# Hybrid layer on one core: state space outputs made transposed, with z as columns and one norm a group

## The chip, the core and the metric

The kernel runs on one core of a Trainium2 chip. Time is device time in microseconds (us), the median of several runs. The engines are TensorE (PE; PEld is its weight load), VectorE (DVE), ScalarE (ACT), GpSimd (POOL) and SyncE (SP), which issues most of the transfers (DMA). Each engine works through its own queue in the order of the program.

## What is computed

One layer over 512 latent tokens and 256 context tokens with 1024 channels: a combined projection, a branch of gated linear attention (GLA, 4 heads), a branch of state space (SSD, 32 heads of 64 channels in 4 groups, chunks of 128 tokens), a merge with gates, and an FFN. The change is in the SSD branch. Cut to that branch, the reference is:

```python
# _ssd_scan, per chunk; a second scan runs backward, and the two outputs are added
cum = jnp.cumsum(ai, axis=1)
seg = cum[:, :, None] - cum[:, None, :]
Lm  = jnp.exp(jnp.where(mask, seg, -jnp.inf))
cb  = jnp.einsum('btgn,bsgn->btsg', ci, bi)
y   = jnp.einsum('btsg,btsge,bsgep->btgep', cb, Lm, xi)
y   = y + jnp.einsum('btgn,bgenp->btgep', ci, S) * jnp.exp(cum)[..., None]
S_new = jnp.exp(cum[:, -1])[..., None, None] * S + ...
# _mixer
o_b = o_b + d_skip * xh
o_b = o_b * silu(z)
o_b = rms_norm(o_b in 4 groups of 512, ssm_norm_w)
y_b = o_b @ w_pb
```

## The kernel before

Weights come by SP's DMA as fp32 and are split into a high part (whi, by ACT, L188) and the rest (wlo, by POOL or DVE, L189). A projection is three matmuls for each block of 128 inputs: whi with the activations' high part, wlo with the high part, whi with the low part. `proj_cols` gives channels on partitions (512 tokens in a row, banks l_ for latents and c_ for context), `proj_rows` gives tokens on partitions (256 channels in a row, banks r_). These banks have the tag mm, four in all; the chains use four others (tag sm).

The SSD branch is done in four groups g. `ssd_proj(g)` projects bm, cm and four blocks of xs with `proj_cols`, puts each through a convolution (cv_ on ACT and DVE, ct_ for its silu) and transposes it to rows (tr_b, tr_x on PE). Then z: in two column halves c, `proj_rows` makes four tiles of 128 tokens, 192 matmuls of 256 columns a group; ACT and DVE write silu(z) into the four tiles z[0] to z[3].

`ssd_chain(g)` makes the states and then, for each chunk n of 128 tokens, the outputs of the group's 8 heads:
- E: the transposed decay matrix of a head, four heads to a tile. SP broadcasts the cumulated decays from DRAM (cdr), DVE adds a bias for each direction (L830), a masked copy joins the two directions (L832), ACT takes the exp (L833), DVE multiplies by cb = B C (L840).
- y: 8 matmuls, E as the weights and 64 columns of x, into one bank (tokens on partitions). yi: two matmuls of 512 columns for what comes from the states ahead and behind.
- DVE scales each yi by exp(cum) and adds it to a tile that POOL made of x and gam (own term and skip, L851), adds the bank and multiplies by z.
- The norm of the chunk: square with its sum on ACT, power on POOL, product with the norm's weights snw on DVE (L866), four transposes on PE (yT), and out of their bank the high part yH by ACT (L871) and the low part yL by DVE (L872).

Order: the matmuls of the chains go through `Early`, which gives them high priority; the scheduler puts them between the matmuls of the projections. Chain g runs beside `ssd_proj(g+1)`, chain 3 beside the gate projections ga and gb. `proj_back` (pb) of a group follows its chain.

## Time and profile before

| | |
|---|---|
| median of three runs | 1442.92 us (1441.3 to 1446.59) |
| the profiled execution | 1443.79 us |
| its span | 1442.0 us |
| mean granted PE clock | 0.981 |
| PE, DVE, ACT, POOL busy | 94%, 61%, 34%, 33% |

The SSD branch lies between about 440 and 990 us. In a timeline a row has the start, the duration, the engine and the line, what is written from what, and in square brackets the idle time ahead of it with what ended it. A matmul's record is longer than the distance to the next one's start, since matmuls are pipelined; where a projection runs without holes, the distance between starts is what one costs. A line that ends in x6 is six instructions in a row.

### The profile page before, as it was taken

Reading aid. Unit: us, or ns where it says so; the run is one execution under the profiler, and the core shown is the slowest. Engines: PE = TensorE matmul, PEld = TensorE weight load, DVE = VectorE, ACT = ScalarE, POOL = GpSimd, SP = SyncE. Lnnn points to the kernel's source line nnn. Section 1 sums busy time; section 2 is a strip of 40 time slices with the busy share of each in tenths; the row PEclk is TensorE's granted clock in tenths of the full one; section 3 lists DMA queues with packets and bytes.
Section 4 is the critical chain, followed back from the end, with each engine's and each line's share of the span. In section 5 each row is a group of like instructions: output and inputs, shape, how many; then the busy total and the mean of one; then the engine's idle time right before and its main releaser. Section 6 shows DMA issues by size and latency. Waiting matters only on the chain.

```text
span 1442.0 us, 19130 instructions
## 1 busy us (share of the span) xinstructions
PE 1357.0 (94%) x7461; PEld 1149.3 (80%) x7461; DVE 882.6 (61%) x1316; ACT 497.1 (34%) x825; POOL 475.3 (33%) x340
## 2 busy tenths in 40 slices
...
GB/s 370 118 264 148 134 88 128 106 103 111 124 78 66 142 103 89 96 88 88 110 74 88 88 110 102 179 179 283 171 88 97 94 102 91 100 102 88 103 103 72
DMA packets 71354, 175.48 MB, mean 122 GB/s; under 512 B 6368, under 2 KB 22880, under 8 KB 71136
## 3 DMA queue, kind: packets, MB, share of 16 engines
...
## 4 chain that ended last, share of the span: by engine, by line
PE 62%; DVE 16%; DMA 11%; issue 5%; POOL 3%; ACT 2%; SPq 0%; POOLq 0%; DVEq 0%; ACTq 0%
DMA E<-cdr 7%; PE gate L1067 3%; PE gate L1068 3%; PE gate L1066 3%; PE up L1067 3%; PE up L1068 3%; PE up L1066 3%; PE db L206 3%; PE db L204 3%; PE db L205 3%; DVE E L830 2%; PE lv L577 2%; PE pb_pb L716 1%; PE pb_pb L715 1%; PE pb_pb L717 1%
## 5 line engine op out<-in xcount | busy, mean ns | idle before, releaser
L341 POOL TENSOR_TENSOR raw_ada<-raw_ada,cs 128x1024 f32<-128x1024 f32 x32 | 67.6, 2113 | 159.4 <-DMA raw_ada<-in_wts_dram 109.2
L170 POOL TENSOR_TENSOR rr_f<-rv_f,negh 128x1 f32<-128x1 f32 x4 | 2.6, 646 | 355.3 <-DVE rv_f L168 355.3
L830 DVE TENSOR_TENSOR E<-E,ebias 128x512 f32<-128x512 f32 x64 | 66.3, 1038 | 56.2 <-DMA E<-cdr 56.0
L386 PE MATMUL r_z<-whi_z,hH 128*128 128x256 f32 x256 | 74.5, 291 | 5.8 <-DVE cv_x L746 3.5
L343 POOL TENSOR_TENSOR raw_ada<-raw_ada 128x512 f32<-128x512 f32 x64 | 78.5, 1227 | 3.0
L388 PE MATMUL r_z<-whi_z,hL 128*128 128x256 f32 x256 | 73.2, 286 | 0.0
L387 PE MATMUL r_z<-wlo_z,hH 128*128 128x256 f32 x256 | 72.9, 285 | 0.0
L1067 PE MATMUL gate<-h2L,whi_gate 128*128 128x512 f32 (+1 forms) x192 | 72.0, 375 | 0.7 <-DVE h2L L1039 0.7
L1066 PE MATMUL gate<-h2H,whi_gate 128*128 128x512 f32 (+1 forms) x192 | 72.3, 377 | 0.0
L1068 PE MATMUL gate<-h2H,wlo_gate 128*128 128x512 f32 (+1 forms) x192 | 71.9, 374 | 0.0
L189 DVE TENSOR_TENSOR wlo_gate<-raw_gate,whi_gate 128x1024 fp32r<-128x1024 f32 x20 | 24.5, 1225 | 73.8 <-ACT whi_gate L188 73.8
L189 POOL TENSOR_TENSOR wlo_xs<-raw_xs,whi_xs 128x1024 fp32r<-128x1024 f32 x16 | 41.2, 2573 | 74.3 <-ACT whi_xs L188 74.3
L1066 PE MATMUL up<-h2H,whi_up 128*128 128x512 f32 x160 | 62.2, 389 | 0.0
L1067 PE MATMUL up<-h2L,whi_up 128*128 128x512 f32 x160 | 62.2, 389 | 0.0
L1068 PE MATMUL up<-h2H,wlo_up 128*128 128x512 f32 x160 | 62.2, 389 | 0.0
L189 DVE TENSOR_TENSOR wlo_down<-raw_down,whi_down 128x1024 fp32r<-128x1024 f32 x18 | 22.0, 1225 | 62.4 <-ACT whi_down L188 62.3
L833 ACT ACTIVATE E<-E 128x512 f32<-128x512 f32 x32 | 20.2, 632 | 112.0 <-DVE E L832 87.8
L1075 DVE TENSOR_TENSOR f<-f,up 128x512 f32<-128x512 f32 x22 | 15.1, 688 | 69.2 <-PE up L1068 68.5
L386 PE MATMUL r_v<-whi_v,hH 128*128 128x256 f32 x192 | 56.8, 296 | 0.0
L189 POOL TENSOR_TENSOR wlo_z<-raw_z,whi_z 128x1024 fp32r<-128x1024 f32 x16 | 39.7, 2484 | 49.1 <-ACT whi_z L188 39.4
L387 PE MATMUL r_v<-wlo_v,hH 128*128 128x256 f32 x192 | 55.8, 291 | 0.0
L388 PE MATMUL r_v<-whi_v,hL 128*128 128x256 f32 x192 | 55.8, 291 | 0.0
...
## 6 DMA issues: line engine op xcount, KB each, us to landing
...
E<-cdr SPq DMA_DIRECT2D x64, 256.0 KB, 3.6
...
```

The lines of the kernel that those rows point to most:

```text
L189: (nc.gpsimd if split_pool[0] else nc.vector).tensor_tensor(lo, raw, hi.bitcast(F32), ALU.subtract)
L204: nc.tensor.matmul(out_, aH, bH, start=start, stop=False)
L205: nc.tensor.matmul(out_, aH, bL, start=False, stop=False)
L341: nc.gpsimd.tensor_tensor(raw, raw, cs[:, :, 0:1].to_broadcast([P, KD, P]), ALU.mult)
L343: nc.gpsimd.tensor_tensor(raw[:, 0:n, :], raw[:, 0:n, :], raw[:, n:2 * n, :], ALU.add)
L386: nc.tensor.matmul(o, hH[:, kk, tk], hi[:, k, :], start=st, stop=False, skip_group_check=True)
L387: nc.tensor.matmul(o, hH[:, kk, tk], lo[:, k, :], start=False, stop=False, skip_group_check=True)
L388: nc.tensor.matmul(o, hL[:, kk, tk], hi[:, k, :], start=False, stop=sp, skip_group_check=True)
L830: nc.vector.tensor_tensor(ed, ed, ebias[:, d, n, hh].unsqueeze(2).to_broadcast([P, EH, P]), ALU.add)
L1066: nc.tensor.matmul(pts[kj][:, tk], hi[:, k, :], h2H[:, k, tk], start=(k == 0), stop=False)
L1067: nc.tensor.matmul(pts[kj][:, tk], hi[:, k, :], h2L[:, k, tk], start=False, stop=False)
L1068: nc.tensor.matmul(pts[kj][:, tk], lo[:, k, :], h2H[:, k, tk], start=False, stop=(k == KD - 1))
```

## The change

- z is projected with `proj_cols` in four blocks of 128 channels, 96 matmuls of 512 columns a group, into one tile of 128 x 4 x 512 with a single buffer (tag z). GLA and the last norm, which used the four buffers of that tag, use quarters of one such tile.
- The outputs are made transposed: channels on partitions. x (or a state) is the weight with 64 columns, E is what streams, 128 tokens wide. Even heads of a pair go to columns 0 to 63 of PE, odd heads to 64 to 127; two heads so fill a 128 x 128 block of the bank.
- What comes from the states is summed in the same bank: cd = exp(cum) C, made by ACT (exp of the broadcast decays) and POOL (product with C), streams against the states. Three buffers (tag cd).
- gam, now with both directions' dt, is put on E's diagonal by a second masked copy, with the mask id8.
- z is multiplied in place by the bank. The square sums over 512 channels are four matmuls with a column of ones (ss). The power, the diagonal matrix dg, the matmul that spreads the norms over the partitions (rrow), the product with the weights and the writing of yH and yL are done once a group, after its last chunk.

```diff
-        z = [ch.tile([P, 512], F32, tag="z", name=f"z_{g}_{i}", bufs=4) for i in range(4)]
-        for c in range(2):
-            banks = proj_rows(lambda kh: ("z", g, c, kh), 4)
-            for i in range(4):
-                pv = banks[i // 2][:, (i % 2) * 256:(i % 2) * 256 + 256]
-                zv = z[i][:, c * 256:(c + 1) * 256]
-                nc.scalar.activation(zv, pv, AF.Tanh, scale=0.5)
-                nc.vector.scalar_tensor_tensor(zv, zv, 1.0, pv, ALU.add, ALU.mult)
+        z = ch.tile([P, 4, SEQ], F32, tag="z", name=f"z_{g}")
+        for j in range(4):
+            lat, _ = proj_cols(("z", g, j), False)
+            nc.scalar.activation(z[:, j, :], lat, AF.Tanh, scale=0.5)
+            nc.vector.scalar_tensor_tensor(z[:, j, :], z[:, j, :], 1.0, lat, ALU.add, ALU.mult)
...
+        def square_sums(n):
+            sq = s2(f"sq{n}")
+            nc.scalar.activation(sq.rearrange("p (j t) -> p j t", t=P), z[:, :, n * P:(n + 1) * P], AF.Square)
+            pt = sm_bank(f"ss_{g}_{n}")
+            for j in range(4):
+                early.matmul(pt[:, 0:1], sq[:, j * P:(j + 1) * P], one, start=(j == 0), stop=(j == 3))
+
+            nc.vector.tensor_scalar(rv4[:, n:n + 1], pt[:, 0:1], 1.0 / (4 * 512), EPS, ALU.mult, ALU.add)
...
+                    cd = ch.tile([P, EH, P], F32, tag="cd", name=f"cd_{g}_{n}_{hf}_{d}", bufs=3)
+                    nc.scalar.activation(cd, ed, AF.Exp)
+                    nc.gpsimd.tensor_tensor(cd, cd, bc[:, 1, tk].unsqueeze(1).to_broadcast([P, EH, P]), ALU.mult)
                     nc.vector.tensor_tensor(ed, ed, ebias[:, d, n, hh].unsqueeze(2).to_broadcast([P, EH, P]), ALU.add)
...
+                nc.vector.copy_predicated(Eh[hf], id8.unsqueeze(1).to_broadcast([P, EH, P]),
+                                          gam[:, hf * EH:(hf + 1) * EH].unsqueeze(2).to_broadcast([P, EH, P]))
...
-            for e_ in range(HPG):
-                early.matmul(py[:, e_ * 64:(e_ + 1) * 64], Eh[e_ // EH][:, e_ % EH, :], xt[:, n, e_ * 64:(e_ + 1) * 64],
-                                 start=True, stop=True)
-            y = s2(f"y{n}")
-            nc.gpsimd.tensor_tensor(v8(y), v8(xt[:, n, :]), b8(gam), ALU.mult)
-            for d, S in ((0, Sf), (1, Sb[n])):
-                pi = sm_bank(f"yi_{g}_{n}_{d}")
-                early.matmul(pi, bc[:, 1, tk], S, start=True, stop=True)
-                yi = s2(f"yi{n}{d}")
-                nc.vector.tensor_tensor(v8(yi), v8(pi), b8(ecum[:, d, n, hs]), ALU.mult)
-                nc.vector.tensor_tensor(y, y, yi, ALU.add)
-            nc.vector.tensor_tensor(y, y, py, ALU.add)
-            nc.vector.tensor_tensor(y, y, z[n], ALU.mult)
+            for hf, term in ((0, 0), (0, 1), (1, 0), (1, 1), (0, 2), (1, 2)):
+                for eh in range(EH):
+                    e_ = hf * EH + eh
+                    es = slice(e_ * 64, (e_ + 1) * 64)
+                    w, m = ((xt[:, n, es], Eh[hf]), (Sb[n][:, es], Ch[hf][1]), (Sf[:, es], Ch[hf][0]))[term]
+                    early.matmul(py[64 * (e_ % 2):64 * (e_ % 2) + 64, (e_ // 2) * P:(e_ // 2 + 1) * P], w, m[:, eh, :],
+                                 start=(term == 0 and e_ < 2), stop=(term == 2 and e_ >= HPG - 2), skip_group_check=True)
...
-            ss = sml.tile([P, 1], F32, tag="ss", name=f"yss_{g}_{n}", bufs=4)
-            nc.scalar.activation(py, y, AF.Square, accum_out=ss)
-            r = rstd_of(ss, 4 * 512, f"y{g}{n}")
-            nc.vector.scalar_tensor_tensor(y, y, r, snw, ALU.mult, ALU.mult)
-            pt = sm_bank(f"yT_{g}_{n}")
-            for j in range(4):
-                early.transpose(pt[:, j * P:(j + 1) * P], y[:, j * P:(j + 1) * P], ident)
-            pv = pt.rearrange("p (j t) -> p j t", t=P)
-            nc.scalar.activation(yH[:, :, tk], pv, AF.Copy)
-            nc.vector.tensor_tensor(yL[:, :, tk], pv, yH[:, :, tk].bitcast(F32), ALU.subtract)
+            nc.vector.tensor_tensor(z[:, :, tk], py.rearrange("p (j t) -> p j t", t=P), z[:, :, tk], ALU.mult)
+            if n > 0:
+                square_sums(n - 1)
+        square_sums(NCH - 1)
+
+        r4 = sml.tile([P, NCH], F32, tag="rr4", name=f"rr_y{g}")
+        nc.gpsimd.tensor_tensor(r4, rv4, negh, ALU.pow)
+        dg = s2("dg")
+        nc.vector.tensor_tensor(dg.rearrange("p (n t) -> p n t", t=P), ident.unsqueeze(1).to_broadcast([P, NCH, P]),
+                                r4.unsqueeze(2).to_broadcast([P, NCH, P]), ALU.mult)
+        pr_ = sm_bank(f"rrow_{g}")
+        early.matmul(pr_, mkr[:, M_ONE - 1, :].bitcast(F32), dg, start=True, stop=True)
+        for j in range(4):
+            zj = z[:, j, :]
+            nc.vector.scalar_tensor_tensor(zj, zj, vecs[:, V_SN + 4 * g + j:V_SN + 4 * g + j + 1], pr_, ALU.mult, ALU.mult)
+            nc.scalar.activation(yH[:, j, :], zj, AF.Copy)
+            nc.vector.tensor_tensor(yL[:, j, :], zj, yH[:, j, :].bitcast(F32), ALU.subtract)
```

How the order moves, at three places. First PE at chunk 1 of group 1 (y_1_1), between the context matmuls of xs_2_0 (c_xs; st is a state's input, ss square sums of chunk 0, cb the next chunk's B C). Before:

```order
L368 MATMUL c_xs_2_0_6150<-hH_91,wlo_xs_2_0_6144 128x256
L364 MATMUL c_xs_2_0_6150<-hH_91,whi_xs_2_0_6143 128x256
L365 MATMUL c_xs_2_0_6150<-hL_92,whi_xs_2_0_6143 128x256
L577 MATMUL y_1_1_5845<-x_1_5017,E_1_1_0_1_5822 128x64 x2
L577 MATMUL yi_1_1_0_5856<-S_f1_1_5802,bc_1_4897 128x512
L577 MATMUL y_1_1_5845<-x_1_5017,E_1_1_0_1_5822 128x64
L577 MATMUL yi_1_1_1_5861<-S_b1_1_5730,bc_1_4897 128x512
L577 MATMUL y_1_1_5845<-x_1_5017,E_1_1_0_1_5822 128x64
L577 MATMUL y_1_1_5845<-x_1_5017,E_1_1_1_1_5830 128x64 x4
L368 MATMUL c_xs_2_0_6150<-hH_91,wlo_xs_2_0_6144 128x256
L364 MATMUL c_xs_2_0_6150<-hH_91,whi_xs_2_0_6143 128x256
```

and after the change:

```order
L578 MATMUL y_1_1_5683<-E_1_1_0_1_5643,x_1_4947 64x128 x2
L578 MATMUL st_1_f2_5708<-xc_f2_0_1_5709,bt_1_4897 128x512
L578 MATMUL y_1_1_5683<-E_1_1_0_1_5643,x_1_4947 64x128
L578 MATMUL ss_1_0_5718<-one_80,sq0_1_5716 128x1
L578 MATMUL y_1_1_5683<-E_1_1_0_1_5643,x_1_4947 64x128
L578 MATMUL cb_1_2_5738<-bc_1_4827 128x128
L578 MATMUL y_1_1_5683<-cd_1_1_0_1_5645,S_b1_1_5551 64x128
L578 MATMUL ss_1_0_5718<-one_80,sq0_1_5716 128x1
L578 MATMUL y_1_1_5683<-cd_1_1_0_1_5645,S_b1_1_5551 64x128
L578 MATMUL ss_1_0_5718<-one_80,sq0_1_5716 128x1
L578 MATMUL y_1_1_5683<-cd_1_1_0_1_5645,S_b1_1_5551 64x128
L578 MATMUL ss_1_0_5718<-one_80,sq0_1_5716 128x1
```

The block was one; now its first eight matmuls (half hf = 0, four heads, two terms; seven of them stand above) have six others between them, and the other sixteen come later.

Second, PE from chain 0's last chunk (y_0_3) to the transposes of group 1 (tr_b, tr_x). Before, from y_0_3 to the z matmuls (r_z) that follow:

```order
L577 MATMUL y_0_3_4859<-x_0_3890,E_0_3_0_1_4836 128x64 x2
L577 MATMUL yi_0_3_0_4870<-S_f3_0_4816,bc_0_3770 128x512
L577 MATMUL y_0_3_4859<-x_0_3890,E_0_3_0_1_4836 128x64
L577 MATMUL yi_0_3_1_4875<-S_b3_0_4591,bc_0_3770 128x512
L577 MATMUL y_0_3_4859<-x_0_3890,E_0_3_0_1_4836 128x64
L577 MATMUL y_0_3_4859<-x_0_3890,E_0_3_1_1_4844 128x64 x4
L386 MATMUL r_z_1_0_0_1_5335<-whi_z_1_0_0_5336,hH_91 128x256
L387 MATMUL r_z_1_0_0_1_5335<-wlo_z_1_0_0_5337,hH_91 128x256
```

and, 50 rows of r_z later:

```order
L387 MATMUL r_z_1_0_0_1_5335<-wlo_z_1_0_1_5391,hH_91 128x256
L388 MATMUL r_z_1_0_0_1_5335<-whi_z_1_0_1_5390,hL_92 128x256
L577 MATMUL yT_0_3_4889<-idt_77,y3_0_4868 128x128 x4
L757 MATMUL tr_b_1_0_4968<-idt_77,ct_b_1_4963 128x128 x4
L757 MATMUL tr_b_1_1_4974<-idt_77,ct_b_1_4963 128x128 x2
L757 MATMUL tr_x_1_0_0_5086<-idt_77,ct_x_1_0_5083 128x128 x4
L386 MATMUL r_z_1_1_0_0_5452<-whi_z_1_1_0_5454,hH_91 128x256
```

After the change, from the end of y_0_3:

```order
L578 MATMUL y_0_3_4766<-cd_0_3_1_0_4758,S_f3_0_4714 64x128 x4
L578 MATMUL ss_0_3_4802<-one_80,sq3_0_4800 128x1 x4
L578 MATMUL rrow_0_4812<-dg_0_4810,mkr_76 128x512
L759 MATMUL tr_b_1_0_4898<-idt_77,ct_b_1_4893 128x128 x4
L759 MATMUL tr_b_1_1_4904<-idt_77,ct_b_1_4893 128x128 x2
L759 MATMUL tr_x_1_0_0_5016<-idt_77,ct_x_1_0_5013 128x128 x4
L759 MATMUL tr_x_1_0_1_5022<-idt_77,ct_x_1_0_5013 128x128 x2
L759 MATMUL tr_x_1_1_0_5094<-idt_77,ct_x_1_1_5091 128x128 x4
L759 MATMUL tr_x_1_1_1_5100<-idt_77,ct_x_1_1_5091 128x128 x2
L759 MATMUL tr_x_1_2_0_5172<-idt_77,ct_x_1_2_5169 128x128 x4
L759 MATMUL tr_x_1_2_1_5178<-idt_77,ct_x_1_2_5169 128x128 x2
L362 MATMUL l_z_1_2_5333<-hH_92,whi_z_1_2_5327 128x512
```

The 54 z matmuls between y_0_3 and what closes the chunk are gone from there, and ss, rrow and all transposes of xs_1_0 to xs_1_2 follow one another; the next z matmul (l_z_1_2) stands behind them.

Third, DVE at the same place (z_1 is the tile of group 1's z, yT holds yL). Before:

```order
L168 TENSOR_SCALAR rv_y03_4884<-yss_0_3_4882 128x1
L781 SCALAR_TENSOR_TENSOR z_1_0_5330<-z_1_0_5330,r_z_1_0_0_0_5334 128x256
L866 SCALAR_TENSOR_TENSOR y3_0_4868<-y3_0_4868,rr_y03_4886,snw_0_4581 128x512
L781 SCALAR_TENSOR_TENSOR z_1_1_5331<-z_1_1_5331,r_z_1_0_0_0_5334 128x256
L830 TENSOR_TENSOR E_1_1_0_1_5822<-E_1_1_0_1_5822,ebias_697 128x512
L832 COPY_PREDICATED E_1_1_0_1_5822<-le8_78,E_1_1_0_0_5819 128x512
L781 SCALAR_TENSOR_TENSOR z_1_2_5332<-z_1_2_5332,r_z_1_0_0_1_5335 128x256
L872 TENSOR_TENSOR yT_0_4580<-yT_0_3_4889,yT_0_4580 128x4x128
L794 TENSOR_SCALAR snw_1_5707<-snw_1_5707 128x512
L750 SCALAR_TENSOR_TENSOR ct_x_1_1_5161<-ct_x_1_1_5161,cv_x_1_1_5152 128x768
L830 TENSOR_TENSOR E_1_1_1_0_5827<-E_1_1_1_0_5827,ebias_697 128x512
L781 SCALAR_TENSOR_TENSOR z_1_3_5333<-z_1_3_5333,r_z_1_0_0_1_5335 128x256
```

and after:

```order
L886 SCALAR_TENSOR_TENSOR z_0_4180<-z_0_4180,vecs_74,rrow_0_4812 128x512 x4
L888 TENSOR_TENSOR yT_0_4450<-z_0_4180,yT_0_4450 128x512
L752 SCALAR_TENSOR_TENSOR ct_x_1_1_5091<-ct_x_1_1_5091,cv_x_1_1_5082 128x768
L888 TENSOR_TENSOR yT_0_4450<-z_0_4180,yT_0_4450 128x512 x2
L752 SCALAR_TENSOR_TENSOR ct_x_1_2_5169<-ct_x_1_2_5169,cv_x_1_2_5160 128x768
L888 TENSOR_TENSOR yT_0_4450<-z_0_4180,yT_0_4450 128x512
L748 SCALAR_TENSOR_TENSOR cv_x_1_3_5238<-l_xs_1_3_5188,vecs_74,cv_x_1_3_5238 128x8x62
L748 SCALAR_TENSOR_TENSOR cv_x_1_3_5238<-c_xs_1_3_5189,vecs_74,cv_x_1_3_5238 128x254
L748 SCALAR_TENSOR_TENSOR cv_x_1_3_5238<-l_xs_1_3_5188,vecs_74,cv_x_1_3_5238 128x8x63
L748 SCALAR_TENSOR_TENSOR cv_x_1_3_5238<-c_xs_1_3_5189,vecs_74,cv_x_1_3_5238 128x255
L780 SCALAR_TENSOR_TENSOR z_1_5260<-z_1_5260,l_z_1_0_5267 128x512
L748 SCALAR_TENSOR_TENSOR cv_x_1_3_5238<-l_xs_1_3_5188,vecs_74,cv_x_1_3_5238 128x8x63
```

z_1's first write stood among chain 0's last steps; now it stands behind the last yL of group 0 and four steps of the convolution cv_x_1_3.

## Rows read from the trace of the kernel before

**Rows 1.** The page: busy us, share, instructions of engines; DMA issues, KB, us to landing.

```profile
PE 1357.0 (94%) x7461; PEld 1149.3 (80%) x7461; DVE 882.6 (61%) x1316; ACT 497.1 (34%) x825; POOL 475.3 (33%) x340
...
E<-cdr SPq DMA_DIRECT2D x64, 256.0 KB, 3.6
```

**Rows 2.** Three stretches: length, busy us of each engine, PE clock, DMA share, GB/s.

```profile
440.00:990.00 550.00, 517.24 (x2863) 425.77 (x2862) 392.98 (x594) 183.70 (x320) 233.56 (x155) 0.99 0.34 110
710.00:715.00 5.00, 3.14 (x19) 2.97 (x18) 2.52 (x6) 4.27 (x10) 2.90 (x2) 0.75 0.50 171
930.00:935.00 5.00, 4.04 (x11) 3.17 (x11) 3.73 (x7) 1.32 (x4) 1.43 (x2) 0.66 0.91 327
```

**Rows 3.** PE's waits, 440 to 990: us in total, times, longest.

```profile
PE yT L577 <- DVE y L866: 9.9, 6, 1.9
...
PE r_z L386 <- DVE cv_x L746: 3.5, 3, 1.5
...
PE r_z L386 <- DVE z L781: 2.3, 2, 1.3
```

**Rows 4.** Timeline of PE: start, us, engine, line, operation, matrices.

```profile
572.77 0.28 PE L387 MATMUL r_z<-wlo_z,hH 128*128 128x256 f32 x1
...
573.96 0.28 PE L388 MATMUL r_z<-whi_z,hL 128*128 128x256 f32 x1
```

**Rows 5.** Timeline of PE in pb of group 3.

```profile
987.32 0.40 PE L715 MATMUL pb_pb<-yT,whi_pb 128*128 128x512 f32 x1
...
989.83 0.39 PE L717 MATMUL pb_pb<-yT,wlo_pb 128*128 128x512 f32 x1
```

**Rows 6.** Timeline of PE at one chunk.

```profile
495.08 1.45 PE L577 MATMUL y<-x,E 128*128 128x64 f32 x12
...
497.28 0.33 PE L577 MATMUL y<-x,E 128*128 128x64 f32 x2
497.45 1.08 PE L577 MATMUL yi<-S_b,bc 128*128 128x512 f32 x2
...
498.50 0.48 PE L361 MATMUL l_bm<-hH,whi_bm 128*128 128x512 f32 x1
```

**Rows 7.** Timeline of PE at transposes.

```profile
581.59 0.82 PE L757 MATMUL tr_b<-idt,ct_b 128*128 128x128 f32 x6
```

**Rows 8.** Timeline of PE around ada matmuls early in the kernel.

```profile
42.74 0.28 PE L364 MATMUL c_misc<-hH,whi_misc 128*128 128x256 f32 x1
42.95 1.06 PE L277 MATMUL ada<-aw,csw 128*32 128x512 f32 x8
...
44.28 0.28 PE L365 MATMUL c_misc<-hL,whi_misc 128*128 128x256 f32 x1
```

**Rows 9.** Groups of DVE, 440 to 1000: shapes, count, busy us, mean ns, idle before.

```profile
L832 DVE COPY_PREDICATED E<-le,E 128x512 f32<-128x512 uint8 x30 | 27.8, 927 | 0.2
L857 DVE TENSOR_TENSOR y<-y,yi 128x512 f32<-128x512 f32 x32 | 25.1, 785 | 2.3 <-POOL y L851 1.2
L856 DVE TENSOR_TENSOR yi<-yi,ecum 128x512 f32<-128x512 f32 x32 | 21.8, 682 | 9.6 <-PE yi L577 9.5
```

**Rows 10.** Groups of ACT and POOL, same stretch.

```profile
L833 ACT ACTIVATE E<-E 128x512 f32<-128x512 f32 x30 | 19.0, 632 | 103.1 <-DVE E L832 78.9 <-PE st_f L577 19.3 <-DVE ada L215 4.4
...
L851 POOL TENSOR_TENSOR y<-x,gam 128x512 f32<-128x512 f32 x16 | 17.6, 1102 | 34.5 <-DVE gam L844 34.4
...
L170 POOL TENSOR_TENSOR rr_y<-rv_y,negh 128x1 f32<-128x1 f32 x16 | 9.7, 607 | 57.4 <-DVE rv_y L168 57.3
```

**Rows 11.** Timeline of DVE at the end of group 0.

```profile
575.10 2.59 DVE L830 TENSOR_TENSOR E<-E,ebias 128x512 f32<-128x512 f32 x1 [0.66 <-DMA E<-cdr]
...
590.98 0.73 DVE L746 SCALAR_TENSOR_TENSOR cv_x<-l_xs,vecs,cv_x 128x504 f32<-128x504 f32 x1
591.63 0.95 DVE L750 SCALAR_TENSOR_TENSOR ct_x<-ct_x,cv_x 128x768 f32<-128x768 f32 x1
```

**Rows 12.** Timeline of POOL there.

```profile
574.75 2.40 POOL L189 TENSOR_TENSOR wlo_z<-raw_z,whi_z 128x1024 fp32r<-128x1024 f32 x1 [3.15 <-ACT whi_z L188]
```

More of the change, by code (lines that the diff above doesn't have):

```diff
@@ L81, in ssd @@
             blk(("xs", g, j), "w_in", 0, 8, C_XS + g * 512 + j * P, P)
-        for c in range(2):
-            for kh in range(2):
-                blk(("z", g, c, kh), "w_in", kh * 512, 4, C_Z + g * 512 + c * 256, 256)
+        for j in range(4):
+            blk(("z", g, j), "w_in", 0, 8, C_Z + g * 512 + j * P, P)
     def pa(pr):
@@ L155, in hybrid_layer_kernel @@
     le8 = cst.tile([P, P], U8, name="le8")
+    id8 = cst.tile([P, P], U8, name="id8")
     one = cst.tile([P, 1], F32, name="one")
@@ L464, in hybrid_layer_kernel @@
     gdr = dr.tile([P, 2, 2, 6, 512], F32, name="gdr")
+    ghs = ch.tile([P, 4, 512], F32R, tag="z", name="gh")
     for d in range(2):
@@ L510, in hybrid_layer_kernel @@
     nc.vector.scalar_tensor_tensor(dt, v, 0.0, lu, ALU.max, ALU.add)
-    dtb = cst.tile([P, 4, 32], F32, name="dtb")
-    nc.vector.tensor_copy(dtb, dt[:, 0:4, 32:64])
+    dts = cst.tile([P, 4, 32], F32, name="dts")
+    nc.vector.tensor_tensor(dts, dt[:, 0:4, 0:32], dt[:, 0:4, 32:64], ALU.add)
     ldt = dt_tile("dt_ln")
@@ L627, in gla_chain @@
             qd.append(q_)
-        S = [ch.tile([P, 2, DV], F32, tag="z", name=f"S_{h}_{n}", bufs=4) for n in range(NCH)]
+        Sall = ch.tile([P, NCH, 2, DV], F32, tag="z", name=f"S_{h}")
+        S = [Sall[:, n] for n in range(NCH)]
         for d, order in ((0, (0, 1, 2, 3)), (1, (3, 2, 1, 0))):
@@ L834, in ssd_chain @@
                 Eh.append(E[1])
-            pcb = sm_bank(f"cb_{g}_{n}")
-            early.matmul(pcb[:, 0:P], bc[:, 0, tk], bc[:, 1, tk], start=True, stop=True)
-            cb = sml.tile([P, P], F32, tag="cb", name=f"cbs_{g}_{n}")
-            nc.scalar.activation(cb, pcb[:, 0:P], AF.Copy)
-            for hf in range(2):
-                nc.vector.tensor_tensor(Eh[hf], Eh[hf], cb.unsqueeze(1).to_broadcast([P, EH, P]), ALU.mult)
-            cbd = sml.tile([P, 1], F32, tag="cbd", name=f"cbd_{g}_{n}")
```

57 lines of the change are left out of this document (30 added, 27 removed).

## The prediction

> **What bounds the kernel now.** I read the page's busy shares first: TensorE (PE) has work for 94% of the span, VectorE (DVE) for 61%, ScalarE (ACT) and GpSimd (POOL) for a third each [rows 1]. The change acts in the state space stage only, so I asked for that stretch: from 440 to 990 us PE is busy 517 of 550 us at a granted clock of 0.99 [rows 2]. So PE's work plus some 33 us of holes is that stage's time. What ends the holes: PE waits 9.9 us in six places for DVE's normalization (y, L866) before the yT transposes, 3.5 us for the convolution (cv_x) and 2.3 us for the evicted z before r_z [rows 3]. I call these 15.7 us the waits that can go. In such a stage, DVE or ACT work that lies beside matmuls is free, matmuls and changes between them cost their full time, and a wait counts from where PE's row of filler matmuls runs out.
>
> **z projected as columns.** Before, 4 groups x 192 matmuls of 256 columns. They start 0.119 us apart (572.77 to 573.96 is ten spacings) [rows 4]: 768 x 0.119 = 91.4 us. After, 4 x 96 of 512 columns, the form that starts 0.228 us apart (987.32 to 989.83, eleven spacings) [rows 5]: 87.6. **-4 us.**
>
> **State space matmuls.** One chunk's y and yi took 495.08 to 498.50, 3.42 us [rows 6]; its four yT transposes are 0.11 us each by a row of six, whose 0.82 holds a tail of 0.16 (a 512-column record of 0.39 is longer by that than its spacing of 0.23) [rows 5, 7]: 0.44. A group of four chunks: 15.4. After, a chunk has 24 matmuls of 128 columns in fp32. Each is two instructions, as a y matmul is (sixteen for eight heads: 12 and two times 2, one of which stands there) [rows 6], and I price one at the 128-column 0.11. Even heads use columns 0 to 63 of the array and odd heads 64 to 127, so a pair may run at once. All paired: 24 x 0.11 = 2.6; the first eight alone, because other work is between them: 3.5. I take 3.1, 12.3 a group. The square sums add 16 matmuls at 2 x 0.11 = 3.5, the row of norms (rrow, 512 columns) 8 x 0.11 = 0.9. 16.7 against 15.4, times four: **+5 us** (0 to 8).
>
> **Changes of tile shape.** In the order of after, st_f, ss and cb stand between single y matmuls, and each of these goes from 128x64 back to 128x128 and again to 128x64. I count 101 round trips more than before. The trace has one kind of them: between matmuls of l_q and l_misc stand ada matmuls in 128x32 tiles. From 42.74 to 44.28 is 1.54 us [rows 8]. In it are one 256-column start (0.12), eight ada instructions (their record of 1.06 less the tail of 0.16) and one 512-column start (0.23): 1.25. So a round trip costs some 0.3. Bounds: 0.15 if half of it belongs to ada's own start, 0.5 if none overlaps. 101 x 0.3 = **+30 us** (15 to 50). The Trainium skill, "TensorEngine Tiling (Array Packing)", section "Tiling Modes", says that a change of the tiling mode drains the TensorE; it gives no price. The trace agrees, with the 0.3 us above. Taken strictly, with nothing overlapped at all, it makes the upper bound of 50, and the sum below 20 higher, 1542.
>
> **The end of a group.** This is the largest term. z is now one tile with a single buffer: z of group g+1 cannot be written (ACT's tanh) until DVE's last yL of group g has read the old one, and yL now stands behind a norm of the whole group. In PE's order nothing but 18 transposes stands between z_1_1 and z_1_2 to fill, and z_1_2 needs the bank that z_1_0's eviction frees. From the end of z_1_1, by mean durations [rows 9, 10]:
> - first eight y_0_3 with four ss and their round trips: 16 x 0.11 + 0.9 + 4 x 0.3 = 3.9;
> - this frees the buffer of the fourth cd (there are three): exp 0.63, E add 0.68, masked copy 0.93, exp 0.63, product with cb 0.68, masked copy for the diagonal 0.93: 8.4;
> - sixteen matmuls 1.8: 10.2;
> - ACT has the exps of three cd of the next chain ahead of the square. The third waits for its E, whose buffer is free at about 9.3 and whose transfer takes 3.6 [rows 1]: 13.5 with the exp; square 0.6, as an exp, ss 0.9, scale and power 0.8, diagonal 0.68, rrow 0.9: 17.4;
> - on DVE four products and four yL at 0.68 (5.4), two ct_x at 0.95 and four cv_x at up to 0.73 [rows 11] that stand between, one z 0.7: 28.3. With a dozen hand-overs, 29 to 30.
>
> PE's own work in it: 3.9 + 1.8 + 0.9 + 0.9 + 18 x 0.11 = 9.5. Idle: 19 at the first two boundaries, 14 at the third, where 22 matmuls of z_3_1 (5 us) stand after the first eight. 52, less the 15.7 that go: **+37 us** (15 to 55). The fourth group has no z behind it, only pb_3: square, ss, power, diagonal, rrow, product, copy and yL are bare, about 6 less the PE work in it: **+5 us** (2 to 8).
>
> **The clock after holes.** After the idle stretches ahead of 712 and 931 the granted clock was 0.75 and 0.66 over 5 us [rows 2], some 1.3 to 1.7 us lost each. With longer holes, two or so at each of four places: **+6 us** (0 to 14).
>
> **What I cost at nothing.** DVE loses two yi products (0.68) and three sums (0.79) a chunk, 3.7, and gains two masked copies (0.93) and a quarter of a diagonal, 2.0 [rows 9]: about 28 us less over 16 chunks. ACT gains 64 exps of 0.63, POOL 64 products of some 1.1 less 16 of 1.1 [rows 9, 10]: 40 and 53 us. Within a group these are hidden: a half chunk's chain is 4.5 us by the list above, plus hand-overs, while PE has 8 to 9 us of projections between the two halves. If that cover is gone, each of 28 places waits. The snw transfers go from SP's queue; nothing waited for them. Gated attention and FFN keep their order; only their buffers have new names.
>
> **Sum.** -4 + 5 + 30 + 37 + 5 + 6 = +79, on the profiled 1443.8: 1522.8. The median stands 0.9 lower: **1522 us**.
>
> **Rivals.**
> 1. *POOL against DVE.* An E add, 0.68 alone, took 2.59 while POOL's wlo_z (2.40, from 574.75) ran [rows 11, 12]. With 53 us more on POOL, and each E now passing DVE, ACT, DVE, ACT, DVE, two such hits make the 4.5 us chain 8.5 and beat the filler. 28 places at 1 to 2 us: +28 to +56, 1550 to 1578. Chance 0.11. The Trainium skill, "SBUF — State Buffer", section "Terms", has the port pair that DVE and GpSimd share as a lock held for a whole instruction; the trace's 2.59, ending 0.5 after wlo_z, agrees.
> 2. *The halves don't run together*: the change doesn't do what it says. 24 x 0.22 = 5.3 a chunk, not 3.1: +35, 1557. Against it: eight 512-column ada instructions in four column tiles took 1.06 [rows 8], where two of yi in the full array take that. Chance 0.05.
> 3. *Cheap shape changes, short boundaries.* If a round trip costs 0.15 or less and DVE clears the boundary in 20 us: -4 + 5 + 12 + 12 + 3 + 3 = +31, range +10 to +45: 1455 to 1488. Chance 0.17.
> 4. *Faster, by DVE's relief.* The 0.3 was all ada's own and a change of shape is free; the six waits on L866 and those before r_z vanish with the work that caused them; boundaries fill as before. -4 + 5 - 15.7, and perhaps 5 of the other holes: 1424 to 1430. It decides where shape changes and boundaries together stay under some 15 us. For it: PE's waits on DVE are real [rows 3]. Against: the single z tile. Chance 0.10. No change (a mix): 0.04.
>
> **How the numbers follow.** Forecast 0.53: 1522, its own range 1490 to 1550. A measurement of this kernel tells about 0.5% (7 us) from no change. The range of 8 in 10 leaves out the cases of rival 4 and no change (0.14) and the far end of rival 1 (0.05): 1455 to 1565. Faster 0.10, same 0.04, slower 0.86.
>
> **What would show it.** (a) z matmuls 0.228 apart, 384 of them. (b) The uninterrupted sixteen y matmuls of a chunk in 1.8 us: if 3.5, the halves do not overlap. (c) Around each ss, st or cb inside y, gaps of 0.3 us a round trip. (d) PE waiting 10 us and more, in sum, from z_1_1 to z_1_2 and at the two like places, the last of it for DVE's z. (e) clock below 0.8 after those holes. (f) POOL busy some 50 us more, DVE 28 less, E add's mean not above 1.1. I am wrong if PE's idle time between 440 and the end of the stage does not grow, or if PE's rows close up around ss.

## The result

The changed kernel takes 1544.01 us (median of four runs, 1543.57 to 1547.71) against 1444.73 for the kernel before on the same chip: a ratio of 1.070, 95% interval 1.067 to 1.073. The forecast was 1522 in a range of 1455 to 1565. The profiled run is 1544.11 us with a span of 1542.2; the mean granted PE clock fell from 0.981 to 0.952.

From the page of the kernel after, the engines' line of part 1 and the clock of the 40 slices (the first is to be read against [rows 1]):

```profile
PE 1425.8 (92%) x7597; PEld 1168.6 (76%) x7597; DVE 890.5 (58%) x1252; ACT 532.0 (34%) x856; POOL 559.6 (36%) x377
...
PEclk8999999999999996999699979998999999999999
```

PE's share of busy time fell by two points while its busy time grew by 69 us. POOL has 84 us more work (475.3 before), DVE 8 more (882.6 before). In slices 16, 20 and 24 of 40 the clock is down to 0.6 to 0.7, in slice 28 to 0.8: these are the ends of the four groups.

PE's waits from 440 to 1090 us (what waits, for whom, us in total, times, longest), against [rows 3]:

```profile
PE y L578 <- DVE E L858: 17.0, 5, 6.9
PE rrow L578 <- DVE dg L880: 11.3, 4, 4.7
PE ss L578 <- ACT sq L795: 11.1, 4, 3.1
PE tr_x L759 <- DVE ct_x L752: 7.1, 6, 1.6
PE l_z L362 <- DVE z L780: 5.2, 3, 1.7
```

The waits before yT and those for cv_x are gone; 52 us of others stand in their place, nearly all at the ends of groups. The timeline of PE at the end of group 0 (columns as in the section on time and profile before; z_1_1 ended at 572.2):

```profile
575.73 0.69 PE L578 MATMUL y<-E,x 128*64 128x128 f32 x4 [3.56 <-DVE E L858]
...
586.73 1.12 PE L578 MATMUL y<-E,x 128*64 128x128 f32 x8 [5.34 <-DVE E L858]
...
593.14 1.86 PE L578 MATMUL ss<-one,sq 128*128 128x1 f32 x8 [2.73 <-ACT sq L795]
597.24 2.05 PE L578 MATMUL rrow<-dg,mkr 128*128 128x512 f32 x2 [2.23 <-DVE dg L880]
...
603.64 0.88 PE L759 MATMUL tr_x<-idt,ct_x 128*128 128x128 f32 x6 [1.65 <-DVE ct_x L752]
...
608.98 0.79 PE L362 MATMUL l_z<-hH,whi_z 128*128 128x512 f32 x1 [1.73 <-DVE z L780]
```

and the granted clock in a stretch of it (columns as in [rows 2]):

```profile
585.00:590.00 5.00, 3.27 (x32) 3.27 (x32) 1.96 (x3) 1.22 (x3) 0.50 (x1) 0.50 0.28 92
```

From the end of z_1_1 to the first matmul of z_1_2 it is 36.8 us. PE waits for 18.4 of them (the idle times of this stretch; one of 1.20 is not shown) and works in the others, mostly at a clock of 0.50, the lower of its two levels (1.2 GHz): from about 575 to 602 without a break; the six tr_x at 603.64 ran at 1.00.

To see how much of a time is work, holes and clock, I add up, over stretches of 5 us, three things for each profiled run: the idle time of PE (stretch less busy), the clock's part (busy x (1 - granted clock)), and the rest, which is PE's work at the upper level of the clock. Here they stand for all kernels, with the number of changes of the array's shape in the program. The time is the median of several runs; the three parts add up to the span of the profiled one, which differs from the median by up to 7 us (e3).

| kernel | time, median | work | idle | clock | shape changes |
|---|---|---|---|---|---|
| before | 1444.7 | 1336 | 85 | 21 | 11 |
| after | 1544.0 | 1375 | 116 | 51 | 213 |
| e1_y_apart | 1557.6 | 1370 | 131 | 54 | 197 |
| e2_few_changes | 1506.3 | 1350 | 114 | 42 | 75 |
| e3_both | 1530.8 | 1348 | 126 | 50 | 71 |
| e5_z_columns | 1462.6 | 1329 | 101 | 31 | 11 |
| e6_cd4 | 1490.9 | 1367 | 87 | 32 | 175 |
| e7_cd4_few_changes | 1483.3 | 1358 | 91 | 33 | 127 |
| e8_no_norm | 1466.1 | 1342 | 93 | 31 | 121 |
| e9_fill | 1514.0 | 1388 | 93 | 31 | 75 |
| e10_no_product | 1449.7 | 1361 | 65 | 21 | 143 |
| e11_one_block | 1470.0 | 1344 | 94 | 35 | 45 |
| e12_dve_product | 1452.6 | 1345 | 83 | 26 | 45 |
| e13_after_no_product | 1528.8 | 1376 | 110 | 40 | 213 |

The change cost 39 us of work, 31 of holes and 30 of clock. The kernel before, timed again beside each set of kernels, took 1444.7 to 1448.8; each ratio below is against the runs of its own set. Differences in us are those of the times; by the ratios, the kernels set against after come out 2 to 7 us lower.

### The profile page after: what moved, and what is told of

It reads as the page before. It is cut to its first block, busy times and chain, and to the rows that moved or that the text cites. A ratio compares the mean times of both kernels' runs of the same rounds, so it can differ in the third digit from the quotient of the medians.

```text
span 1542.2 us, 19398 instructions
## 1 busy us (share of the span) xinstructions
PE 1425.8 (92%) x7597; PEld 1168.6 (76%) x7597; DVE 890.5 (58%) x1252; ACT 532.0 (34%) x856; POOL 559.6 (36%) x377
## 5 line engine op out<-in xcount | busy, mean ns | idle before, releaser
L839 POOL TENSOR_TENSOR cd<-cd,bc 128x512 f32<-128x512 f32 x64 | 110.0, 1737 | 70.2 <-ACT cd L838 70.2
L840 DVE TENSOR_TENSOR E<-E,ebias 128x512 f32<-128x512 f32 x64 | 83.2, 1317 | 47.2 <-ACT cd L838 46.9
L838 ACT ACTIVATE cd<-E 128x512 f32<-128x512 f32 x64 | 37.6, 624 | 75.1 <-PE y L578 49.8
L362 PE MATMUL l_z<-hH,whi_z 128*128 128x512 f32 x128 | 53.8, 421 | 5.2 <-DVE z L780 5.2
L205 PE MATMUL db<-wlo_down,fH 128*128 128x512 f32 x142 | 56.4, 397 | 0.0
L189 POOL TENSOR_TENSOR wlo_pb<-raw_pb,whi_pb 128x1024 fp32r<-128x1024 f32 x12 | 28.7, 2389 | 75.9 <-ACT whi_pb L188 75.9
L206 PE MATMUL db<-whi_down,fL 128*128 128x512 f32 x142 | 55.9, 393 | 0.0
```

The lines of the kernel that those rows point to most:

```text
L189: (nc.gpsimd if split_pool[0] else nc.vector).tensor_tensor(lo, raw, hi.bitcast(F32), ALU.subtract)
L205: nc.tensor.matmul(out_, aH, bL, start=False, stop=False)
L206: nc.tensor.matmul(out_, aL, bH, start=False, stop=stop)
L362: nc.tensor.matmul(lat, hi[:, k, :], hH[:, k, 0:SEQ], start=st, stop=False)
L839: nc.gpsimd.tensor_tensor(cd, cd, bc[:, 1, tk].unsqueeze(1).to_broadcast([P, EH, P]), ALU.mult)
L840: nc.vector.tensor_tensor(ed, ed, ebias[:, d, n, hh].unsqueeze(2).to_broadcast([P, EH, P]), ALU.add)
```

## The experiments

**Where do the holes come from: z's single tile?** The prediction put the long group ends down to z of the next group standing behind the norm. In e1 the product of outputs and z goes to another tile (the squares read it there):

```diff
-            nc.vector.tensor_tensor(z[:, :, tk], py.rearrange("p (j t) -> p j t", t=P), z[:, :, tk], ALU.mult)
+            nc.vector.tensor_tensor(yL[:, :, tk], py.rearrange("p (j t) -> p j t", t=P), z[:, :, tk], ALU.mult)
...
-            zj = z[:, j, :]
+            zj = yL[:, j, :].bitcast(F32)
```

> The kernel after, but the product of outputs and z goes to the tile of yL and the norm works there, so that z's tile is free as soon as the last chunk's product has read it, and z of the next group no longer stands behind the norm (y is rounded to fp32r on the way, so the low part is lost). Theory: the three group ends cost about 31 us of idle PE and 30 us of low clock, and most of both hangs on z's single tile; with the third z block ahead of the norm's matmul PE has 5 to 11 us of filler there, and 25 to 45 us come back: 1500 to 1519. Rival: the norm once a group sets the end by itself, whatever buffer z has: under 12 us come back, 1532 or more.

Measured: 1557.6, ratio 1.076 (1.073 to 1.078): slower still. PE's waits for E rose from 17.0 to 44.8 us, and the timeline at the end of group 1 shows where:

```profile
730.87 0.70 PE L578 MATMUL y<-E,x 128*64 128x128 f32 x4 [9.25 <-DVE E L858]
...
741.87 1.12 PE L578 MATMUL y<-E,x 128*64 128x128 f32 x8 [5.35 <-DVE E L858]
...
750.99 0.79 PE L362 MATMUL l_z<-hH,whi_z 128*128 128x512 f32 x1 [0.83 <-DVE z L780]
```

z_2_2 (the l_z at 750.99) now follows the square sums at once, as intended, without rrow and 18 transposes ahead of it. But the second half of the last chunk comes as late as before (741.87 against 742.23 in the kernel after), and in PE's order the third z block stands behind it. So the holes only moved ahead of y_1_3. (The edit could have a cost of its own, since yL must be free of the last group's pb before the first product; in its trace this product never waits for pb.) The theory of z's tile fell. The rival's bound held (1532 or more), but what PE waits for longest is here not the norm, but E.

**What does a change of shape cost?** e2 queues the square sums, state inputs and cb behind the eighth y matmul of a chunk:

```diff
-                early.matmul(pt[:, 0:1], sq[:, j * P:(j + 1) * P], one, start=(j == 0), stop=(j == 3))
+                with behind():
+                    early.matmul(pt[:, 0:1], sq[:, j * P:(j + 1) * P], one, start=(j == 0), stop=(j == 3))
...
+                if (hf, term) == (0, 1):
+                    half[0] = mm.ins
```

(the state inputs and cb are queued in the same way).

> The kernel after, but the square sums, state inputs and cb matmuls are queued behind the first eight y matmuls of a chunk, so that the array changes its shape 75 times and not 213: 69 round trips fewer, same work. Theory: one costs 0.35 us: -24 us, 1520. Rival: most of that is the single matmuls' own latency, and a round trip costs 0.1 or less: -7 us or less, 1537 or more.

Measured: 1506.3, ratio 1.039 (1.036 to 1.041), 38 us less. The same block (eight y matmuls, st_f, cb, four ss) of chunk 2 of group 0, in the kernel after:

```profile
550.08 0.44 PE L578 MATMUL y<-E,x 128*64 128x128 f32 x4
...
551.50 0.43 PE L578 MATMUL y<-E,x 128*64 128x128 f32 x2
551.87 0.38 PE L578 MATMUL ss<-one,sq 128*128 128x1 f32 x2
552.18 0.43 PE L578 MATMUL y<-E,x 128*64 128x128 f32 x2
...
555.35 0.39 PE L369 MATMUL c_xs<-hH,wlo_xs 128*128 128x256 f32 x1
```

and in e2:

```profile
551.71 0.66 PE L578 MATMUL y<-E,x 128*64 128x128 f32 x8
...
552.73 1.12 PE L578 MATMUL st_f<-xc_f,bt 128*128 128x512 f32 x2
...
554.73 0.48 PE L363 MATMUL l_xs<-hL,whi_xs 128*128 128x512 f32 x1
```

5.27 us against 3.02 (550.08 to 555.35, 551.71 to 554.73) with six round trips less: 0.375 us each. 69 of them are 26 us, and by that the work fell; the rest came from holes and clock. Over the whole program, from after to e11 below, 168 changes (84 round trips) less are 31.6 us of work less, again 0.376 each. The price holds more than the change itself: a y matmul that stands alone also loses its overlap with the other column half, an estimated 0.1 of the 0.375 (two instructions at 0.11 us each alone [rows 7] and 0.06 in the long run of chunk 2's second half, whose rows stand further below). The theory held, with a gain above its figure.

**Both.** e3 has both edits.

> Both edits of the two kernels before. Theory: the two costs lie in different places and add: -50 to -70 us, 1475 to 1494. Rival: the time is set by the chain of steps on DVE, ACT and POOL, and what PE saves in one place it waits in the other: no more than the larger of the two alone.

Measured: 1530.8, ratio 1.056 (1.054 to 1.059). Work is that of e2, holes and clock are near those of e1. The loss of e1 (14) and the gain of e2 (38) would make 1520; 11 us more are lost. The theory does not fit; the rival's bound (no more than the larger gain alone) held, though e1 by itself had lost and not won.

**z as columns by itself.** e5 is the kernel before with

```diff
-        for c in range(2):
-            banks = proj_rows(lambda kh: ("z", g, c, kh), 4)
...
+        for j in range(4):
+            lat, _ = proj_cols(("z", g, j), False)
+            nc.scalar.activation(z[j], lat, AF.Tanh, scale=0.5)
+            nc.vector.scalar_tensor_tensor(z[j], z[j], 1.0, lat, ALU.add, ALU.mult)
```

> The kernel before with its z projection alone made as columns (4 blocks of 96 matmuls of 512 columns, four separate tiles; the values are then those of other tokens and channels, the work is the same). Theory: 384 x 0.228 for 768 x 0.119: -4 us, 1440. Rival: z's first products come later, since a block is complete for all channels only at the end, and the end of a group waits longer: 0 or slower.

Measured: 1462.6, ratio 1.0085 (1.0057 to 1.0113), slower. The work fell, by 7 us; 16 us of holes and 10 of clock came. The largest of PE's waits from 440 to 1010, and the group end with the longest of them:

```profile
PE yT L576 <- DVE y L862: 24.8, 11, 6.0
```

```profile
723.13 0.39 PE L365 MATMUL l_z<-hH,wlo_z 128*128 128x512 f32 x1
729.52 1.08 PE L576 MATMUL yT<-idt,y 128*128 128x128 f32 x4 [6.01 <-DVE y L862]
...
732.39 1.20 PE L714 MATMUL pb_pb<-yT,whi_pb 128*128 128x512 f32 x2
```

The chain's last transposes (yT) waited 9.9 us in all before [rows 3], now 24.8: in this order they stand behind the last z block, and only ten transposes come between them and the pb that needs them (732.39), where before half of z came after them. Why the scheduler's order has each step of the chain some matmuls later I did not find out; that part is open. The arithmetic of the edit was right, its effect on the order was not in the sum.

**The chain's pace: three cd buffers.** In the kernel after, ACT's exps for cd and DVE's adds on E wait like this from 440 to 1090:

```profile
ACT cd L838 <- PE y L578: 49.8, 25, 6.1
```

```profile
DVE E L840 <- ACT cd L838: 43.4, 22, 5.7
```

A half chunk takes two cd buffers. With three, the fourth exp waits for the first eight y matmuls; E's add overwrites what that exp reads and waits behind it; so the second half's chain starts when the first half's matmuls are done. In the trace the eight halves of group 0 start at 500.1, 514.1, 525.7, 539.2, 550.1, 564.6, 575.7 and 586.7, one every 11 to 14.5 us, and the projections run out before the chain does. e6:

```diff
-                    cd = ch.tile([P, EH, P], F32, tag="cd", name=f"cd_{g}_{n}_{hf}_{d}", bufs=3)
+                    cd = ch.tile([P, EH, P], F32, tag="cd", name=f"cd_{g}_{n}_{hf}_{d}", bufs=4)
```

(and six s2 buffers for seven).

> The kernel after with four cd buffers for three (and six s2 buffers for seven, which pays for the room). New theory, since e1 freed z's tile and won nothing: with three cd buffers the exp of a chunk's fourth cd waits for the first eight y matmuls, E's add, which overwrites what that exp reads, waits behind it, and so the two halves of a chunk run one after the other; the chain of a group outlasts its filler, and the holes at the group's end follow from that. With four, the holes and the low clock at the three group ends shrink by more than half: -35 to -55 us, 1489 to 1509. Rival: the norm once a group and the tile of z make the holes: -12 us at most, 1532 or more.

Measured: 1490.9, ratio 1.031 (1.028 to 1.033), 53 us less. The two waits, again, in e6:

```profile
ACT cd L838 <- PE y L578: 16.6, 21, 3.5
```

```profile
DVE E L840 <- ACT cd L838: 11.3, 11, 4.7
```

49.8 became 16.6, and 43.4 became 11.3; group 0's last half is done at 572.4 (590.4 in the kernel after). Idle time is back at that of before (87 against 85). Of the 53 us, 8 are work: in the order that came out, the array changes its shape 38 times less.

e7 has the edits of e6 and of e2:

> Four cd buffers, and the square sums, state inputs and cb behind the first eight y matmuls. Theory: both costs are real and add: 0.375 us for each of some 60 round trips less (22 us) on top of the buffers' gain: 1455 to 1485. Rival: once the chain is short, the changes of shape no longer matter, since they fill what were holes: no more than 5 us under the run with four buffers alone.

Measured: 1483.3, ratio 1.025 (1.022 to 1.028), only 8 us less than with the buffers alone. The time lies at the edge of the theory's range, but the gain is neither the theory's 22 nor the rival's 5 at most: with four buffers the second half's sixteen matmuls come close behind the first half, so that square sums, state inputs and cb, queued behind the eighth, now often stand among the sixteen. 24 round trips went (175 changes to 127), 9 us of work.

**The norm.** e8 leaves out squares, square sums, power, dg and rrow:

```diff
-            nc.vector.scalar_tensor_tensor(zj, zj, vecs[:, V_SN + 4 * g + j:V_SN + 4 * g + j + 1], pr_, ALU.mult, ALU.mult)
+            nc.vector.tensor_scalar(zj, zj, vecs[:, V_SN + 4 * g + j:V_SN + 4 * g + j + 1], None, ALU.mult)
```

> The kernel after with the norm left out (no squares, square sums, power, diagonal, rrow; the weights alone are multiplied). Theory of the buffers: 64 square sums with some 64 round trips at 0.375 us and 0.2 us each of work go (37 us), and the waits on the norm at the four group ends (22 us idle, at half clock partly), but the wait of the second half of each last chunk stays (5 to 7 us a group): 1470 to 1495, and PE still waits 15 us or more for E. Rival: the norm is what PE waits for at the end of a group: 1455 or less and no long wait left.

Measured: 1466.1, ratio 1.014 (1.010 to 1.018), between the two ranges. 33 us of work, 23 of holes, 19 of clock less than after. PE's waits for E go on, with one of 9.3 us:

```profile
PE y L578 <- DVE E L858: 12.1, 7, 9.3
```

12.1 us in all, a little under the expected 15. The norm so has a large part in the time, and is not all of what PE waits for. What norm and buffers save together was not run, so the two savings (78 and 53) may overlap.

**The clock.** e9 is e2 with matmuls nobody reads in the holes at the end of each group:

```diff
+        def fill(pd, ins, k):
+            with tc.issue_after(ins):
+                for i in range(k):
+                    early.matmul(pd, mkr[:, 0, :], hH[:, i % KD, 0:SEQ], start=True, stop=True)
...
+                    if pd is not None:
+                        fill(pd, half[0], 18)
...
+        fill(pd, mm.ins, 12)
+        fill(pd, square_sums(NCH - 1), 9)
```

> The kernel with few changes of shape (e2, 1506) with matmuls of 512 columns whose results nobody reads, put on PE where it waits at the end of each group: 18 after the first eight y matmuls of chunk 3, 12 after the other sixteen, 9 after the last square sums, about 9 us of added work a group. Theory: the low clock (26 us lost between 440 and 1100) comes from the holes, and PE's few matmuls in this stretch, which are part of the chain, run at half speed; with PE kept busy the clock stays up there and the added work lies in the holes: 10 to 20 us less, 1486 to 1496. Rival: the clock costs nothing, because the chain waits for DVE, ACT and POOL there: 1503 to 1515.

Measured: 1514.0, ratio 1.047 (1.044 to 1.049), 8 us more than e2. The end of group 0:

```profile
570.25 0.66 PE L578 MATMUL y<-E,x 128*64 128x128 f32 x8 [1.22 <-DVE E L872]
...
573.35 3.28 PE L578 MATMUL fill<-hH,mkr 128*128 128x512 f32 x13
576.90 0.66 PE L578 MATMUL y<-E,x 128*64 128x128 f32 x8 [0.27 <-DVE E L872]
...
597.49 0.77 PE L362 MATMUL l_z<-hH,whi_z 128*128 128x512 f32 x1 [2.48 <-DVE cv_x L748]
```

```profile
575.00:580.00 5.00, 4.73 (x44) 3.72 (x44) 2.67 (x5) 2.03 (x4) 1.20 (x1) 1.00 0.50 191
```

The same place in e2:

```profile
580.03 1.12 PE L578 MATMUL y<-E,x 128*64 128x128 f32 x8 [4.50 <-DVE E L866]
...
602.29 0.79 PE L362 MATMUL l_z<-hH,whi_z 128*128 128x512 f32 x1 [1.73 <-DVE z L780]
```

With PE kept busy the clock stays at 1.00 up to 590, where e2's matmuls take twice as long from 580 on (eight of y 1.12 us for 0.66): the holes bring it down. In e9 too it falls to 0.50 at the end of the stretch, after holes of 1.67 and 2.28 us that were not filled. But from the end of what precedes y_0_3 to z_1_2 it is 28.5 us (569.03 to 597.49), against 30.1 in e2 (572.22 to 602.29): the clock's part of this stretch fell by 5.4 us, the stretch by 1.6. In a hole the chain waits for other engines, and a matmul at half speed mostly takes time that PE would have waited. Over the whole kernel the fill is more work than it gives back (38 us added, 33 of idle and clock gone). So the 30 us in the column "clock" are, at this place at least, mostly holes under another name; the rival's range held.

**POOL's product.** e10 is e7 with the product of cd and C left out, e13 is the kernel after with the same line left out:

```diff
-                    nc.gpsimd.tensor_tensor(cd, cd, bc[:, 1, tk].unsqueeze(1).to_broadcast([P, EH, P]), ALU.mult)
```

> The kernel with four cd buffers and few changes of shape (1483) with the product of cd and C on POOL left out (64 of 1.64 us). Theory: POOL's product slows DVE's steps on E (masked copy 1.58 us against 0.93 in the kernel before, add 1.12) and is in the chain itself; without it these go back to 0.9 and 0.75, and PE's waits for E (24.9 us) fall under 10: 1455 to 1468. Rival: the steps on DVE are slow for another reason (ACT's or the transfers' use of the memory) and the product is hidden: no more than 6 us less, and the masked copy stays above 1.4.

> The kernel after, three cd buffers and all changes of shape, with the product of cd and C on POOL left out; PE's order at the group ends is that of after. Theory: the two halves of each chunk still run one after the other, so most of the holes at the group ends stay, and only the slower steps on DVE get better: 15 to 35 us less than 1544, 1509 to 1529. Rival: the slow steps are the cause, and three buffers would do without them: 1490 or less, and PE's waits for E under 5 us.

Measured: e10 1449.7, ratio 1.0017 (1.0001 to 1.0034), 34 us less than e7; e13 1528.8, ratio 1.056 (1.051 to 1.062), 15 less than after (19 by the ratios). The masked copy and the add on E, by form (shapes, count, busy us, mean ns, idle before), the add in the kernel before, then both in the kernel after, with POOL's product from the page's part 5:

```profile
L830 DVE TENSOR_TENSOR E<-E,ebias 128x512 f32<-128x512 f32 x59 | 59.4, 1008 | 54.6 <-DMA E<-cdr 54.5
```

```profile
L840 DVE TENSOR_TENSOR E<-E,ebias 128x512 f32<-128x512 f32 x61 | 80.1, 1329 | 43.6 <-ACT cd L838 43.4
L842 DVE COPY_PREDICATED E<-le,E 128x512 f32<-128x512 uint8 x31 | 49.2, 1586 | 0.4
```

```profile
L839 POOL TENSOR_TENSOR cd<-cd,bc 128x512 f32<-128x512 f32 x64 | 110.0, 1737 | 70.2 <-ACT cd L838 70.2
```

in e10:

```profile
L846 DVE TENSOR_TENSOR E<-E,ebias 128x512 f32<-128x512 f32 x60 | 46.6, 779 | 20.4 <-ACT cd L845 20.4
...
L848 DVE COPY_PREDICATED E<-le,E 128x512 f32<-128x512 uint8 x31 | 28.1, 913 | 0.2
```

and in e13:

```profile
L839 DVE TENSOR_TENSOR E<-E,ebias 128x512 f32<-128x512 f32 x61 | 52.2, 870 | 52.3 <-ACT cd L838 51.9
...
L841 DVE COPY_PREDICATED E<-le,E 128x512 f32<-128x512 uint8 x31 | 28.8, 929 | 0.4
```

PE's waits for E in e10 (24.9 us in e7), and in e13:

```profile
PE y L578 <- DVE E L865: 0.8, 1, 0.8
```

```profile
PE y L578 <- DVE E L857: 17.3, 4, 6.0
```

1.59 us for the masked copy beside the product, 0.91 and 0.93 without it, as in [rows 9]; the add 1.33, then 0.78 and 0.87 (1.01 before). POOL's product may be stretched too: 1.74 us in the mean, where the shortest of the 64 took 1.29 and the like product of before 1.10 [rows 10]; no run has it without DVE's steps beside it. The Trainium skill, "SBUF — State Buffer", section "Terms", has the port pair of DVE and GpSimd as an exclusive lock for a whole instruction; these numbers agree with engines that hold each other up, but do not show the lock itself. e13 keeps the halves one behind the other, and PE still waits 17.3 us for E: slow steps and three buffers are two causes. Without the slow steps alone most of the holes stay (110 us idle for 116, e13); with the fourth buffer alone they go back to 87 (e6); with both, and the order of e2, 65 are left (e10).

**One block, and the product on DVE.** e11 queues ss, st and cb behind all 24 matmuls of a chunk, with four cd buffers; e12 adds DVE for the product:

```diff
-                if (hf, term) == (0, 1):
+                if (hf, term) == (1, 2):
                     half[0] = mm.ins
...
-                    nc.gpsimd.tensor_tensor(cd, cd, bc[:, 1, tk].unsqueeze(1).to_broadcast([P, EH, P]), ALU.mult)
+                    nc.vector.tensor_tensor(cd, cd, bc[:, 1, tk].unsqueeze(1).to_broadcast([P, EH, P]), ALU.mult)
```

(the first hunk against e7 is e11, both are e12).

> Four cd buffers, and the square sums, state inputs and cb queued behind all 24 y matmuls of a chunk, so that these are one run: one change of shape there and back for each chunk. Theory: 0.375 us for each of the round trips that were left in the second half (about 40 less): 15 us less than 1483, 1465 to 1472, if PE's wait for the second half's E does not grow. Rival: with the whole chunk in one run the first half's matmuls no longer come early, cd's buffers and cb come later, and the waits for E eat it: 1478 or more.

> The kernel with four cd buffers and one block of y matmuls a chunk (1470), with the product of cd and C on DVE and not on POOL. Theory: what costs is that POOL and DVE slow each other; on DVE the product takes 0.7 us (44 us in all), the masked copies fall back from 1.58 to 0.93 and E's add to 0.78, so DVE's busy time stays about the same and the chain no longer passes POOL: 1450 to 1465. Rival: DVE is now the engine that sets the chain's pace, each half chunk has 1.4 us more on it, and the order spreads the chunks out again: 1475 or more.

Measured: e11 1470.0, ratio 1.017 (1.014 to 1.020), 13 us less than e7, by work alone (1344 for 1358); e12 1452.6, ratio 1.0033 (1.0010 to 1.0057), 17 less again (19 by the ratios). Steps on E and the product in e12:

```profile
L846 DVE TENSOR_TENSOR cd<-cd,bc 128x512 f32<-128x512 f32 x60 | 55.4, 924 | 12.9 <-ACT cd L845 12.9
L847 DVE TENSOR_TENSOR E<-E,ebias 128x512 f32<-128x512 f32 x60 | 47.5, 791 | 0.0
...
L849 DVE COPY_PREDICATED E<-le,E 128x512 f32<-128x512 uint8 x31 | 33.0, 1071 | 0.1
```

```profile
PE y L578 <- DVE E L866: 4.3, 6, 1.3
```

The product takes 0.92 us on DVE where POOL took 1.74 in the kernel after; the add is at 0.79, the masked copy at 1.07, nearly back at 0.93. PE waits 4.3 us for E. With four buffers, one block and the product on DVE the transposed form costs what the kernel before costs, to 0.3%; none of the kernels run beats that one.

## Why the prediction was right in its range and where its steps failed

- **z as columns, -4.** The matmuls cost a little less than priced: e5 has 7 us less work. That this part alone makes the kernel slower by 0.9%, through the order, was not in the sum.
- **State space matmuls, +5.** Right. The uninterrupted sixteen, the whole second half of a chunk:

```profile
564.64 0.66 PE L578 MATMUL y<-E,x 128*64 128x128 f32 x8
565.13 0.61 PE L578 MATMUL y<-cd,S_b 128*64 128x128 f32 x8
565.57 1.04 PE L578 MATMUL y<-cd,S_f 128*64 128x128 f32 x16
566.54 0.51 PE L363 MATMUL l_z<-hL,whi_z 128*128 128x512 f32 x1
```

  32 instructions from 564.64 to 566.54, 1.90 us with one entry into the shape: 0.06 each, half of the 0.11 of a single one. The two column halves run together, so rival 2 is out. 39 us of work in all, less 38 for changes of shape, plus 4 to 7 for z, leave 5 to 8; the term is known only as this remainder.
- **Changes of shape, +30.** Right in kind, a little small: 101 x 0.375 = 38. The bounds (15 to 50) held. The 0.3 from one place with another tile shape was a fair reading; the overlap that single matmuls lose, part of the 0.375, the prediction had half in the term before.
- **Group ends, +37 and +5, and the clock, +6.** Together 48 (52 less 15.7 is 36, not 37); measured 61. Singly the terms were further off: 42 of holes were priced and 31 measured, 6 of clock priced and 30 measured. The prediction priced 29 to 30 us for the first end, 19 of them idle; 36.8 were measured, 18.4 of them idle. Where it expected a short dip of the clock, PE ran at 0.50 for most of the stretch, so that holes showed as slow matmuls. By e9 the low clock itself cost little: kept up, it gave back 1.6 us at that place. The sum of both terms was short by 13 us. The chain's steps were slower than priced: masked copies at 1.59 us and adds at 1.33, not 0.93 and 0.68. Without POOL's product, e13 has 17 us less of holes and clock than after, so these steps can account for the 13; how much of it lies in the steps at the ends was not measured.
- **The cause of the long ends** is the step that failed. "z is now one tile with a single buffer" was named as what holds PE; e1, with three cd buffers, freed it and won nothing. What makes the ends is that the chain outlasts the projections, and for this the runs show two causes. One was in the prediction's own list (the fourth cd waits for its buffer), but as a step of the last chunk; it sets the pace of all 16 chunks, and one buffer more is worth 53 us (e6). The other is the next point. The norm once a group, the prediction's other reason, has a share: without it 42 us of holes and clock go (e8). How much of that is the same as the buffers' share is open.
- **What was costed at nothing.** POOL's products were to be hidden at 1.1 us each, +53 us of POOL, and DVE was to have 28 us less. POOL has 84 more, its products taking 1.74 us each, and DVE 8 more, since its masked copies and adds take longer beside them: sign (f) did not come true (the add's mean is 1.33, above 1.1). With four buffers the product costs 34 us (e10), with three 15 (e13). Rival 1 had this mechanism and the chance of 0.11, but the wrong place: the half chunks inside a group hardly wait (0.8 us once and 0.4 once); the slower steps add up and come due at the end of the group.
- Rivals 3 and 4 are out: a round trip is not cheap, and the waits that went were replaced.

So the sign and the size came from the right places (changes of shape, ends of groups), and the explanation of the larger one was wrong. That its size came near is in part luck: the list of steps that priced the ends holds the chain that really ran, under another cause, and too much for holes stood against too little for the clock.
